# Token rows loaded last, the first x tile scaled in three pieces, a smaller warm-up tile and drawn offsets in the order of a hybrid attention block

## The chip, the cores and the metric

One core of one Trainium2 chip. The metric is the device time of one execution in microseconds; the kernel before has a median of 430.17 us in 3 runs (429.69 to 430.26). Engines are named as in the profile: PE (TensorE's matmuls), PEld (its weight loads), DVE (VectorE), ACT (ScalarE), POOL (GpSimd) and SP (SyncE, which issues most DMAs).

## The reference

The kernel computes one pre-norm residual layer for 512 tokens of width 1024 in float32. With h = rmsnorm(x) * g, one combined projection h @ w_in gives latents, gates and indexer inputs:

```python
h = rmsnorm(x, norm_g[l])
(q_lat, c_kv, k_rope, z_a, q_b, k_b, v_b, z_b,
 q_idx, k_idx, w_idx, gate_a, gate_b) = jnp.split(h @ w_in[l], cuts, axis=-1)
...
merged = (jax.nn.sigmoid(gate_a) * (y_a @ w_o_a[l])
          + jax.nn.sigmoid(gate_b) * (y_b @ w_o_b[l]))
x = x + merged @ w_out[l]
```

Branch a is latent attention: eight heads, queries from a normalised latent of 384 (q_lat), keys and values from one of 256 (c_kv), a shared rotary key, a mask by chunks of 64 tokens. Branch b is attention over selected keys: an indexer of eight small heads scores all keys, each query keeps its 128 best, and a relative position bias is added. Each branch is gated with SiLU, and the sum passes an output projection, the residual and a final rmsnorm.

## The kernel before, in words

**How the order is made.** The work is written as some sixty Python generators ("threads"), each of which yields steps: an engine (or a choice of engines) with an estimated duration, the tiles it writes and those it reads. `Flow.run` (L180) is a list scheduler that runs when the program is built: it keeps a modelled time for each engine, asks for each thread's next step when it could start (`Flow.start`, L163), and emits the step with the smallest key, `s + BIAS * t.prio` with BIAS = 0.01 (L201), ties settled by the thread's priority. What it emits is the fixed order of each engine's queue. On the chip every engine then runs its own queue strictly in that order and waits on semaphores for its inputs. Steps with a choice (DVE or POOL, DVE or ACT) go to the engine that finishes first by the model.

**Precision.** Each product is done as three matmuls of operands split in a high and a low part (`mm3`, L395): high part by a cast (`act`, L305: ACT's CAST at L292, or ACTIVATE at L301 when it scales), low part by a subtraction on DVE or POOL (`lo_part`, L371, at L318 or L320; `split_scaled`, L375, at L329). All matmuls of this kind stand at L390, transposes at L407.

**The start** is where most of the change lies. `setup` (L472) issues the first load of the indexer weight (w_qi, 256 columns) from ACT's queue, writes two constants on DVE (neghalf, and junk with 512 columns) and loads the exponential table. `warm_up` (L481) multiplies junk, read as bfloat16, with itself: seven matmuls of 512 columns. `loads` (L516) issues on SP the eight tiles of x transposed (xT, 128 channels by 512 tokens each, k = 0 to 7), and with them the weights w_qi (256 columns for each k) and w_kvl (328 columns for each k: the kv latent, the indexer key, the rotary key and the indexer's head weights); then the four tiles of w_ql (the q latent). After pair kp = XAT = 1 of xT, that is between k = 3 and k = 4, it stands still for `x_squares` (L552): eight loads of x by token rows (128 tokens by 512 channels), whose squares are summed on ACT (L560, into junk), added in pairs on DVE, and raised to -1/2 on POOL (L368) to give rstd, one number a token. Four transposes on PE (L568) lay rstd along the free dimension, and ACT copies it to rbc (L570).

`early_x` (L595) scales each xT tile by the norm's gain into a high and low part; `early_w` (L603) splits w_qi and w_kvl for each k, then w_ql. `early_mm` (L616) runs on PE for each k six matmuls of 384 columns (the indexer queries, two banks, tokens 128 to 511) and twelve of 328 columns (the kv latents, one bank for each token tile); then the q latents, 96 matmuls of 384 columns. None of these needs rstd, which is applied to the results afterwards: `take_qi` (L716), `latent` (L681). The normalised tiles h (`normed`, L657), on which all other projections run, need rbc, and so do the rope tables' loads on POOL (L496 to L498), which wait for it.

**The rest.** Projections, attention heads, top-k selection (48 pairs of MAX8 and MATCH_REPLACE8 on DVE) and the output products follow, interleaved by the scheduler: a `fetcher` loads weight tiles ahead into four raw buffers, a `splitter` splits them, a `multiplier` fills PE with projections while heads wait for DVE and ACT. Seven strips of products end the kernel (`output`, L1751), followed by the final rmsnorm and eight stores.

Of the kernel before, what the change touches and what calls it, by code (L numbers as in the profile page):

```python
# [2 lines left out]

# [9 lines left out]
BF16 = mybir.dt.bfloat16  # L13
AF = mybir.ActivationFunctionType
# [111 lines left out]


class Thread:
    def __init__(self, gen, prio):
        self.gen, self.prio, self.req, self.alive = gen, prio, None, True  # L130


class Flow:
# [9 lines left out]
    def __init__(self):  # L143
# [3 lines left out]
        self.port = 0.0  # L147
        self.threads = []

    def spawn(self, gen, prio):  # L150
        t = Thread(gen, prio)
        self.threads.append(t)
        self.advance(t, None)
        return t
# [25 lines left out]
    def run(self, stop=None):  # L180
        while self.threads:
            if stop and stop():
                return
            moved = False
            for t in sorted(self.threads, key=lambda t: t.prio):
                if isinstance(t.req, Get):
                    b = t.req.pool.give(t.req)
                    if b is not None:
                        self.advance(t, b)
                        moved = True  # L190
                elif isinstance(t.req, Until) and t.req.cond():
                    self.advance(t, None)
                    moved = True
            if moved:
                continue
            best = None
            for t in self.threads:
                if isinstance(t.req, Step):
                    for i, (eng, dur, emit) in enumerate(t.req.options):
                        s = self.start(t.req, eng)  # L200
                        key = (s + BIAS * t.prio, t.prio)  # L201
                        if len(t.req.options) > 1:
                            fin = s + dur + {"POOL": self.pbias if t.req.pbias is None else t.req.pbias, "ACT": t.req.abias}.get(eng, 0.0)
# [12 lines left out]
            if eng == "SP":  # L216

                self.free["SP"] = s + 0.05
                self.hw = max(self.hw, s) + (0.65 if step.ins and step.outs else 0.475)
                self.dma = max(self.dma, self.hw + 0.65) + dur  # L220
                end = self.dma + (2.2 if step.ins and step.outs else 1.0) + step.late
            else:
                self.free[eng] = end = s + dur
                if self.shares(step, eng):
                    self.port = end
                if step.moves:
                    self.dma = max(self.dma, end + (1.0 if eng == "POOL" else 0.8)) + step.moves
                    end = self.dma + 1.0
            for b in step.ins:
                b.r = b.reads[eng] = max(b.r, end)  # L230
            for b in step.outs:
                b.w = max(b.w, end)
                b.written, b.by = True, eng
            self.advance(t, None)


RAW_LAG = {"DVE": 0.125, "POOL": 0.1, "ACT": 0.1}
BIAS = 0.01
TC_ARGS = {}


@with_exitstack
def tile_block(ctx: ExitStack, tc: tile.TileContext, a: dict, out: bass.AP, bias_dram: bass.AP):
# [211 lines left out]
    kpe = [fixed(f"kpe{c}", [68, S], F32R) for c in "hl"]  # L455
    mask = [fixed(f"mask{i}", [P, P * (i + 1)]) for i in range(NT)]
    junk = fixed("junk", [P, S])
    warm = fixed("warm", [P, 8])
    ss8 = [fixed(f"ss{t}", [P, 2]) for t in range(NT)]
    rstd = fixed("rstd", [P, NT])  # L460
    rb = fixed("rb", [64, NH])
    rbs = fixed("rbs", [64, NH], F32R)
    TOK = [slice(t * P, (t + 1) * P) for t in range(NT)]
    LO, HI = slice(0, 256), slice(256, 512)
    SCORED = slice(P, S)
    SWAP = [(k + 16) % 32 for k in range(32)]
    done = set()

# [3 lines left out]
    def setup():  # L472

        rq = yield slot("er")
        yield act_dma(rq.all.f[:, :256], a["w_qi"][0][:, :256])
        eraw["q", 0] = rq.all.f[:, :256], True
        yield memset("DVE", neghalf.all, -0.5)
        yield memset("DVE", junk.all, 0.0)
        yield act(warm.all, neghalf.all, AF.Exp)

    def warm_up():  # L481

        ps = yield bank("pv")
        z = junk.tile.bitcast(BF16)
        for _ in range(NWARM):
            yield pe(0.43, [ps.all], [junk.all], lambda: nc.tensor.matmul(
                ps.tile, z[:, :P], z[:, :S], start=True, stop=True))
        put(ps)

    def setup_pool():  # L490
# [25 lines left out]
    def loads():  # L516
# [32 lines left out]
                eraw["ql", 2 * kp + c] = r[:, QR * c : QR * c + QR], c == 1  # L549
        done.add("loads")  # L550

    def x_squares():  # L552
        tiles = []

        def squares():
            for t in range(NT):
                for half in range(2):
                    yield Until(lambda: len(tiles) > 2 * t + half)
                    xn = tiles[2 * t + half]
                    yield act(junk.all, xn.all.f, AF.Square, accum=ss8[t][:, half : half + 1])  # L560
                    put(xn)
            ss = yield Get(SMALL)
            for t in range(NT):
                yield tt(ss[:, t : t + 1], ss8[t][:, 0:1], ss8[t][:, 1:2], ALU.add)
# [19 lines left out]
    def split_w(raw, w, dst, key, cls="w", cap=None, release=False, early=False):  # L584
# [7 lines left out]
            put(raw.buf)  # L592
        dst[key] = (hi, lo)

    def early_x():  # L595
        for k in range(NK):
            yield Until(lambda: k in xt)
            hi = yield slot("xg")
            lo = yield slot("xg")
            yield from split_scaled(hi.all, lo.all, xt[k].all.f, normg[:, k : k + 1])  # L600
            xg[k] = (hi, lo)

    def early_w():  # L603
# [12 lines left out]
    def early_mm():  # L616
# [2 lines left out]
            qi_ps.append((yield bank("e")))  # L619
        for _ in range(NT):  # L620
            kv_ps.append((yield bank("e")))
        for k in range(NK):
            yield Until(lambda: k in xg and k in ewq)

# [1 line left out]
            w = [cut(ewq[k], slice(m * P, m * P + P)) for m in range(2)]  # L626
            if k == 0:

                for cw, cx in ((0, 0), (1, 0), (0, 1)):
                    for m in range(2):  # L630
                        yield mm(qi_ps[m][:, SCORED], [(w[m][cw], xk[cx])], not (cw or cx), False)
# [1259 lines left out]
NORM = ('DVE', 'POOL')  # L1891
NORM_B = ('DVE', 'ACT')
NORM_BIAS = -0.5
NWARM = 7
XAT = 1
QPOOL = 1
PHCAP = 8
WCAP = 8
# [95 lines left out]
```

## Time and profile before

| | |
|---|---|
| median of 3 runs | 430.17 us (429.69 to 430.26) |
| the profiled execution's own time | 429.84 us |
| its span, first to last instruction | 428.1 us |
| mean granted TensorE clock | 0.994 |
| busy: PE, DVE, ACT, POOL | 415.9, 379.3, 264.6, 118.7 us |
| DMA | 65.89 MB, mean 154 GB/s |

A row of the timeline gives start, duration, engine, line, operation, tiles written and read, and behind a bracket the idle time of the engine just before and what ended it. In a list of waits the three numbers are the total, the count and the longest. In a table of stages each engine has its busy time and, after an x, its instructions, in the order PE, PEld, DVE, ACT, POOL. A group of instructions has its busy time, then the mean duration of one in ns. Because matmuls overlap, the start-to-start distance of rows says more of PE than a row's length.

### The profile page before, as it was taken

Reading aid. Unit: us, or ns where it says so; the run is one execution under the profiler, and the core shown is the slowest. Engines: PE = TensorE matmul, PEld = TensorE weight load, DVE = VectorE, ACT = ScalarE, POOL = GpSimd, SP = SyncE. Lnnn points to the kernel's source line nnn. Section 1 sums busy time; section 2 is a strip of 40 time slices with the busy share of each in tenths; the row PEclk is TensorE's granted clock in tenths of the full one; section 3 lists DMA queues with packets and bytes.
Section 4 is the critical chain, followed back from the end, with each engine's and each line's share of the span. In section 5 each row is a group of like instructions: output and inputs, shape, how many; then the busy total and the mean of one; then the engine's idle time right before and its main releaser. Section 6 shows DMA issues by size and latency. Waiting matters only on the chain.

```text
span 428.1 us, 7167 instructions
## 1 busy us (share of the span) xinstructions
PE 415.9 (97%) x2303; PEld 363.9 (85%) x2303; DVE 379.3 (89%) x840; ACT 264.6 (62%) x595; POOL 118.7 (28%) x144
## 2 busy tenths in 40 slices
PE   8899999999999999999999999999999999999993
PEld 6899978888888888888799988998998888888882
DVE  4599599999999999999879898988789767999995
ACT  5985876656472676448564678494598534336624
POOL 1247857544545648510000001000010002001112
PEclk9999999999999999999999999999999999999997
DMA  8964334736318630472354435615522887448205
GB/s 261 394 221 155 107 99 128 196 107 171 96 53 229 172 116 3 132 200 99 100 141 144 152 95 136 165 52 177 150 85 80 293 334 253 160 132 278 94 2 196
DMA packets 30277, 65.89 MB, mean 154 GB/s; under 512 B 4648, under 2 KB 5688, under 8 KB 30240
## 3 DMA queue, kind: packets, MB, share of 16 engines
q1 hardware_dynamic: 29264, 64.08, 48.5%
q0 software_dynamic: 832, 1.22, 1.0%
q8 instruction: 18, 0.29, 0.3%
q14 instruction: 19, 0.16, 0.1%
q10 hardware_dynamic: 144, 0.13, 0.1%
HBM read 50.49 MB, written 4.21 MB: 128 GB/s over the span
## 4 chain that ended last, share of the span: by engine, by line
PE 55%; DVE 22%; DMA 8%; ACT 6%; issue 5%; SPq 1%; POOL 1%; POOLq 0%; DVEq 0%; ACTq 0%
PE ps L390 49%; PE ps L407 4%; DMA raw<-w_out 3%; DVE mask L791 3%; DVE sm L790 3%; ACT s_p L301 2%; DVE s_mg L318 2%; DVE s_wsum L318 1%; DMA s_sig<-bias_scratch 1%; DVE sm L1412 1%; DMA raw<-w_kvl 1%; DMA s_op<-kpel 1%; DVE s_wo L318 1%; SPq L417 1%; DVE s_w L318 1%
## 5 line engine op out<-in xcount | busy, mean ns | idle before, releaser
L390 PE MATMUL ps<-s_h,s_w 128*128 128x512 f32 (+1 forms) x732 | 169.9, 379 | 0.0
L390 PEld LDWEIGHTS ps<-s_h,s_w 128*128 128x128 f32 x732 | 127.9, 189 | 22.1 <-DVE s_w L318 0.2
L292 ACT CAST s_w<-raw 128x512 fp32r<-128x512 f32 (+3 forms) x124 | 71.1, 591 | 21.3 <-DVE raw L318 12.5
L320 POOL TENSOR_TENSOR s_w<-raw,s_w 128x512 fp32r<-128x512 f32 (+2 forms) x40 | 50.1, 1263 | 121.5 <-ACT s_w L292 75.9
L318 DVE TENSOR_TENSOR s_w<-raw,s_w 128x512 fp32r<-128x512 f32 (+2 forms) x84 | 54.9, 667 | 8.5 <-ACT s_w L292 8.0
L390 PE MATMUL ps<-s_ys,s_w 128*128 128x512 f32 x192 | 43.7, 389 | 0.0
L390 PEld LDWEIGHTS ps<-s_ys,s_w 128*128 128x128 f32 x192 | 36.0, 188 | 7.5
L390 PE MATMUL ps<-s_w,s_xg 128*128 128x328 f32 (+1 forms) x192 | 32.5, 323 | 0.5 <-DVE s_w L318 0.5
L390 PE MATMUL ps<-s_wo,s_mg 128*128 128x512 f32 (+1 forms) x156 | 33.0, 373 | 0.0
L390 PEld LDWEIGHTS ps<-s_w,s_xg 128*128 128x128 f32 x192 | 31.5, 188 | 0.8 <-DVE s_w L318 0.8
L390 PEld LDWEIGHTS ps<-s_wo,s_mg 128*128 128x128 f32 x156 | 27.6, 188 | 5.2
L301 ACT ACTIVATE s_p<-s_p,sm 128x128 f32<-128x128 f32 (+3 forms) x56 | 29.2, 551 | 3.9 <-DVE sm L1509 3.8
L318 DVE TENSOR_TENSOR s_ph<-ps,s_ph 128x384 fp32r<-128x384 f32 (+1 forms) x48 | 27.0, 592 | 0.6
L301 ACT ACTIVATE s_p<-ps,sm 128x128 f32<-128x128 f32 (+3 forms) x32 | 16.8, 527 | 17.1 <-DVE sm L1412 16.5
L791 DVE MATCH_REPLACE8 mask<-sm,mask 128x256 f32<-128x256 f32 (+2 forms) x48 | 25.8, 540 | 0.0
L790 DVE MAX8 sm<-mask 128x8 f32<-128x256 f32 (+2 forms) x48 | 25.2, 546 | 0.1
L292 ACT CAST s_ph<-ps 128x384 fp32r<-128x384 f32 (+1 forms) x48 | 23.0, 516 | 1.9 <-PE ps L407 1.5
L407 PE MATMUL ps<-ident,s_p 128*128 128x128 f32 x160 | 23.3, 274 | 0.3 <-ACT s_p L301 0.3
L390 PE MATMUL ps<-s_ph,vv 128*128 128x512 f32 (+3 forms) x128 | 23.3, 318 | 0.2 <-DVE s_ph L318 0.2
L390 PEld LDWEIGHTS ps<-s_ph,vv 128*128 128x128 f32 x128 | 20.8, 188 | 2.5 <-DVE s_ph L318 0.4
L351 POOL TENSOR_SCALAR s_p<-s_p,sm 128x128 f32<-128x128 f32 (+3 forms) x32 | 17.3, 544 | 15.6 <-DVE sm L1389 15.4
L407 PEld LDWEIGHTS ps<-ident,s_p 128*128 128x128 f32 x160 | 18.7, 140 | 3.3 <-ACT s_p L301 0.5
(191 smaller groups left out, 750.5 us busy)
## 6 DMA issues: line engine op xcount, KB each, us to landing
raw<-w_out SPq DMA_DIRECT2D x18, 512.0 KB, 4.0
s_op<-s_op SPq DMA_DIRECT2D x36, 128.0 KB, 2.4
raw<-w_ga SPq DMA_DIRECT2D x8, 512.0 KB, 4.5
raw<-w_gb SPq DMA_DIRECT2D x8, 512.0 KB, 4.0
raw<-w_o SPq DMA_DIRECT2D x16, 256.0 KB, 3.7
s_x<-xT SPq DMA_DIRECT2D x8, 256.0 KB, 5.6
s_xn<-x SPq DMA_DIRECT2D x8, 256.0 KB, 5.5
raw<-w_za SPq DMA_DIRECT2D x4, 512.0 KB, 5.0
```

The costliest lines, as they stand in the source:

```text
L292: nc.scalar.copy(dst.ap, src.ap)
L301: nc.scalar.activation(dst.ap, src.ap, func, **kw)
L318: opts.append(("DVE", 0.07 + 0.00104 * x.n, lambda: nc.vector.tensor_tensor(dst.ap, x.ap, y.ap, op=op)))
L320: opts.append(("POOL", 0.15 + 0.0021 * x.n, lambda: nc.gpsimd.tensor_tensor(dst.ap, x.ap, y.ap, op=op)))
L351: lambda: nc.gpsimd.tensor_scalar(dst.ap, x.ap, s.ap, 1.0, ALU.mult, ALU.mult)))
L390: nc.tensor.matmul(ps.ap, l.ap, r.ap, start=start and i == 0, stop=stop and i == len(pairs) - 1, skip_group_check=more)
L407: nc.tensor.transpose(d.ap, s.ap, ident.tile)
L417: return Step([("SP", n / 360000.0, lambda: nc.sync.dma_start(d, s))], bufs(dst), bufs(src))
L790: yield Step([("DVE", t, lambda: nc.vector.max(m8.tile, work.tile))], [m8], [work])
L791: yield Step([("DVE", t, lambda: nc.vector.match_replace(work.tile, m8.tile, work.tile, MARK))], [work], [m8])
L1412: yield Step([("DVE", 0.07 + 0.00104 * n, lambda: nc.vector.tensor_reduce(mx.tile[:, 1:2], ps.tile[:, :n], op=ALU.max, axis=AX.X, negate=T ...
```

## The change

1. `XAT` goes from 1 to 3: the eight token-row loads and what hangs on them stand behind all eight xT tiles with their w_qi and w_kvl loads, and ahead of w_ql.
2. The squares of the token rows may run on ACT or DVE (`square_sum`), each into its own accumulator, over the tile itself in place of junk. In the order that results six run on ACT and two on DVE.
3. The first xT tile is scaled in three pieces (tokens 256 to 511, 128 to 255, 0 to 127) in place of one; the first indexer matmuls (high times high) run by pieces of 256 and 128 columns.
4. The warm-up reads a new tile, zeros, of 128 float32 columns (256 in bfloat16): 15 matmuls of 256 columns in place of 7 of 512; junk is no longer cleared.
5. Each thread gets an offset drawn between 0 and 0.01 (`NUDGE`, seed `DRAW` = 0), added to its key. It changes the order of all queues, and with it which engine some steps with a choice get: over the whole program DVE has 11 instructions more, ACT 4 and POOL 3 fewer. The matmuls are the same but for the warm-up and the split of the first ones.

```diff
-    def __init__(self, gen, prio):
-        self.gen, self.prio, self.req, self.alive = gen, prio, None, True
+    def __init__(self, gen, prio, nudge):
+        self.gen, self.prio, self.nudge, self.req, self.alive = gen, prio, nudge, None, True
...
-        t = Thread(gen, prio)
+        t = Thread(gen, prio, self.draw.random() * NUDGE)
...
-                        key = (s + BIAS * t.prio, t.prio)
+                        key = (s + BIAS * t.prio + t.nudge, t.prio)
...
+    PIECES = (slice(256, S), slice(P, 256), slice(0, P))
...
+        yield memset("DVE", zeros.all, 0.0)
         yield memset("DVE", neghalf.all, -0.5)
-        yield memset("DVE", junk.all, 0.0)
         yield act(warm.all, neghalf.all, AF.Exp)
...
-        z = junk.tile.bitcast(BF16)
+        z = zeros.tile.bitcast(BF16)
         for _ in range(NWARM):
-            yield pe(0.43, [ps.all], [junk.all], lambda: nc.tensor.matmul(
-                ps.tile, z[:, :P], z[:, :S], start=True, stop=True))
+            yield pe(WARM, [ps.all], [zeros.all], lambda: nc.tensor.matmul(
+                ps.tile[:, :256], z[:, :P], z, start=True, stop=True))
...
+    def square_sum(xn, dst):
+
+        x = xn.all.f
+        step = act(x, x, AF.Square, accum=dst.all)
+        step.options.append(("DVE", 0.19 + 0.00104 * x.n, lambda: nc.vector.tensor_tensor_reduce(
+            x.ap, x.ap, x.ap, op0=ALU.mult, op1=ALU.add, scale=1.0, scalar=0.0, accum_out=dst.tile)))
+        step.pair = True
+        return step
...
-                    yield act(junk.all, xn.all.f, AF.Square, accum=ss8[t][:, half : half + 1])
+                    yield square_sum(xn, ss8[t, half])
...
+            if k == 0:
+
+                for piece in PIECES:
+                    yield act(hi[:, piece], xt[k].all.f[:, piece], AF.Copy, scale=normg[:, k : k + 1])
+                    first_x[piece.start] = hi
+                yield stt(lo.all, xt[k].all.f, normg[:, k : k + 1], hi.all.f, ALU.mult, ALU.subtract)
+            else:
+                yield from split_scaled(hi.all, lo.all, xt[k].all.f, normg[:, k : k + 1])
...
+        yield Until(lambda: 0 in ewq)
+        for i, piece in enumerate(PIECES[:2]):
+            yield Until(lambda: piece.start in first_x)
+            for m in range(2):
+                yield mm(qi_ps[m][:, piece], [(ewq[0][0][:, m * P : m * P + P], first_x[piece.start][:, piece])], not i, False)
...
-                for cw, cx in ((0, 0), (1, 0), (0, 1)):
+                for cw, cx in ((1, 0), (0, 1)):
...
-NWARM = 7
-XAT = 1
+NWARM = 15
+WARM = 0.22
+XAT = 3
```

More of the change, by code (lines that the diff above doesn't have):

```diff
@@ L1 @@
 import math
+import random
 from contextlib import ExitStack
@@ L148, in __init__ @@
         self.threads = []
+        self.draw = random.Random(DRAW)
     def spawn(self, gen, prio):
-        t = Thread(gen, prio)
+        t = Thread(gen, prio, self.draw.random() * NUDGE)
         self.threads.append(t)
@@ L238 @@
 BIAS = 0.01
+NUDGE = 0.01
+DRAW = 0
 TC_ARGS = {}
@@ L457, in tile_block @@
     junk = fixed("junk", [P, S])
+    zeros = fixed("zeros", [P, P])
     warm = fixed("warm", [P, 8])
-    ss8 = [fixed(f"ss{t}", [P, 2]) for t in range(NT)]
+    ss8 = {(t, h): fixed(f"ss{t}{h}", [P, 1]) for t in range(NT) for h in range(2)}
     rstd = fixed("rstd", [P, NT])
@@ L563, in squares @@
             for t in range(NT):
-                yield tt(ss[:, t : t + 1], ss8[t][:, 0:1], ss8[t][:, 1:2], ALU.add)
+                yield tt(ss[:, t : t + 1], ss8[t, 0].all, ss8[t, 1].all, ALU.add)
             yield from small_pow(rstd.all, ss[:, :NT], 1.0 / D)
@@ L593, in split_w @@
         dst[key] = (hi, lo)
+    first_x = {}
     def early_x():
@@ L599, in early_x @@
             lo = yield slot("xg")
-            yield from split_scaled(hi.all, lo.all, xt[k].all.f, normg[:, k : k + 1])
+            if k == 0:
[5 more added lines that the diff above has]
+                yield from split_scaled(hi.all, lo.all, xt[k].all.f, normg[:, k : k + 1])
             xg[k] = (hi, lo)
@@ L627, in early_mm @@
             if k == 0:
-                for cw, cx in ((0, 0), (1, 0), (0, 1)):
+                for cw, cx in ((1, 0), (0, 1)):
                     for m in range(2):
-                        yield mm(qi_ps[m][:, SCORED], [(w[m][cw], xk[cx])], not (cw or cx), False)
+                        yield mm(qi_ps[m][:, SCORED], [(w[m][cw], xk[cx])], False, False)
             else:
```

## The prediction

> **What bounds the kernel now.** I read the page first, then who waited for whom on PE, then the timeline of the start, then stages.
>
> ```profile
> span 428.1 us, 7167 instructions
> PE 415.9 (97%) x2303; PEld 363.9 (85%) x2303; DVE 379.3 (89%) x840; ACT 264.6 (62%) x595; POOL 118.7 (28%) x144
> ```
>
> PE is idle for 428.1 - 415.9 = 12.2 us of the span. The waits of PE say where idle time can be won:
>
> ```profile
> PE ps L407 <- POOL rstd L368: 1.8, 1, 1.8
> PE ps L486 <- DVE junk L444: 1.5, 1, 1.5
> PE ps L390 <- DVE s_w L318: 0.5, 1, 0.5
> PE ps L390 <- ACT s_xg L301: 0.3, 1, 0.3
> PE ps L407 <- ACT s_p L301: 0.3, 1, 0.3
> PE ps L1430 <- DMA s_op<-kpel: 0.2, 1, 0.2
> PE ps L390 <- DVE s_ph L318: 0.2, 1, 0.2
> ```
>
> The first four, 4.1 us, lie before 25 us; the last three, 0.7 us, are all that the remaining 400 us hold. The matmuls are the same in both kernels but for the warm-up and two more in the first step, so the time is set by when PE gets going, by how rarely it stops in the first 30 us, and by whether the new order keeps the rest as full. The start:
>
> ```profile
> 0.94 0.48 DVE L444 MEMSET junk<- 128x512 f32 x1
> 1.48 3.17 PE L486 MATMUL ps<-junk 128*128 128x512 bf16 x7 [1.48 <-DVE junk L444]
> 3.90 0.41 ACT L292 CAST s_w<-s_er 128x256 fp32r<-128x256 f32 x1 [1.24 <-DMA s_er<-w_qi]
> 4.22 0.72 ACT L301 ACTIVATE s_xg<-s_x,normg 128x512 fp32r<-128x512 f32 x1
> 4.99 2.15 PE L390 MATMUL ps<-s_xg,s_w 128*128 128x384 f32 x6 [0.34 <-ACT s_xg L301]
> 5.15 0.47 ACT L292 CAST s_w<-s_er 128x328 fp32r<-128x328 f32 x1 [0.22 <-DMA s_er<-w_kvl]
> 5.65 0.50 DVE L318 TENSOR_TENSOR s_w<-s_er,s_w 128x328 fp32r<-128x328 f32 x1
> 6.42 0.72 ACT L301 ACTIVATE s_xg<-s_x,normg 128x512 fp32r<-128x512 f32 x1 [0.80 <-DMA s_x<-xT]
> 6.97 1.96 PE L390 MATMUL ps<-s_w,s_xg 128*128 128x328 f32 x12
> 7.04 0.76 ACT L292 CAST s_w<-s_er 128x256 fp32r<-128x256 f32 x2
> 7.17 0.75 DVE L329 SCALAR_TENSOR_TENSOR s_xg<-s_x,normg,s_xg 128x512 fp32r<-128x512 f32 x1 [1.02 <-ACT s_xg L301]
> 7.84 0.83 DVE L318 TENSOR_TENSOR s_w<-s_er,s_w 128x256 fp32r<-128x256 f32 x2
> 8.77 1.23 PE L390 MATMUL ps<-s_xg,s_w 128*128 128x384 f32 x6
> 9.84 1.95 PE L390 MATMUL ps<-s_w,s_xg 128*128 128x328 f32 x12
> 11.62 1.20 PE L390 MATMUL ps<-s_xg,s_w 128*128 128x384 f32 x6
> ```
>
> A step of the contraction (k) is six matmuls for the indexer and twelve for the kv latents. Undisturbed it takes 11.62 - 8.77 = 2.85 us: 1.07 for the six, 1.78 for the twelve (0.149 each). Step 0 runs its six at 0.33 each, so PE was still at half speed there.
>
> ```profile
> 17.42 0.19 ACT L301 ACTIVATION_READ_ACCUMULATOR junk<-s_xn 128x1 f32 x1
> 17.51 0.71 ACT L301 ACTIVATE s_xg<-s_x,normg 128x512 fp32r<-128x512 f32 x1
> 18.16 1.04 POOL L368 TENSOR_TENSOR rstd<-rstd,neghalf 128x4 f32<-128x4 f32 x1
> 19.17 0.63 POOL L421 DMA_DIRECT2D ropec<-ropec  x1
> 19.26 0.65 PE L407 MATMUL ps<-ident,rstd 128*128 128x128 f32 x4 [1.83 <-POOL rstd L368]
> 19.67 1.31 PE L390 MATMUL ps<-s_xg,s_w 128*128 128x384 f32 x6
> 22.25 0.72 ACT L301 ACTIVATE s_xg<-s_x,normg 128x512 fp32r<-128x512 f32 x1
> 24.49 1.93 PE L390 MATMUL ps<-s_w,s_xg 128*128 128x328 f32 x11 [0.52 <-DVE s_w L318]
> 30.13 12.17 PE L390 MATMUL ps<-s_w,s_xg 128*128 128x328 f32 x71
> ```
>
> Here the eight loads of x's token rows and their eight squares stand between steps 3 and 4: ACT reaches the fifth x tile only at 17.51, PE waits 1.83 us and later 0.52. The last row starts with the twelve matmuls of step 7, at 30.13.
>
> **The change part by part.** *Token rows behind the other loads (XAT 3).* Steps 1 to 6 and the first six matmuls of step 7 take 6 x 2.85 + 1.07 = 18.17 us of PE. In the trace they take 30.13 - 8.77 = 21.36. Of the 3.19 us between, the four transposes of rstd stay (19.67 - 19.26 = 0.41 of PE); **2.78 us of stalls go**, if the loads of steps 4 to 7 keep ahead of PE, and they do: with eight loads and eight squares less in front of them each comes earlier than before.
>
> What is late next is rstd itself. In the new order its transposes stand in PE's queue after the six matmuls of step 6. The same bytes lie ahead of the last token tile as lay ahead of the last x tile, which had landed at 22.25 at the latest. A square (0.54 to its accumulator read) and the tail from that read to PE (19.26 - 17.42 = 1.84) give rstd at 22.25 + 0.54 + 1.84 = 24.6. PE comes there at about 25.3 (below). So the wait is hidden with 0.7 us to spare, and each 0.1 us beyond that would be paid in full. The loads of w_ql stay behind the token tiles; on POOL the two rope loads and the mask rows wait for rstd and move from 19.17 to about 26 us, still long ahead of the rope at 53.84 (its row stands below). Two of the eight squares go to DVE.
>
> ```profile
> L1509 DVE CUSTOM_DVE_ANT_0 s_p<-ps,s_p 128x512 f32<-128x512 f32 x8 | 5.4, 674 | 0.0
> 24.00:50.00 26.00, 25.51 (x154) 25.38 (x155) 21.74 (x38) 19.05 (x47) 16.65 (x21) 1.00 0.44 133
> 70.00:200.00 130.00, 129.60 (x683) 110.93 (x682) 128.96 (x331) 77.34 (x186) 67.10 (x78) 1.00 0.48 133
> 48.56 1.03 PE L407 MATMUL ps<-ident,s_latraw 128*128 128x128 f32 x8
> 53.84 0.68 DVE L318 TENSOR_TENSOR s_tmp<-ps,ropec 32x512 f32<-32x512 f32 x1
> ```
>
> By the first row two such reductions cost DVE 1.4 us, before 23 us, where it has holes. Then everything that needs rstd or its broadcast starts some 6 us later (transposes at 25.4 instead of 19.26): the eight normalised tiles, the kv latents. Their first user on PE comes after the w_ql matmuls, at 48.56 before and about 47 now. DVE has 26 - 21.74 = 4.3 us free between 24 and 50; the splits of steps 4 to 7 leave that stretch (about 3.3 us) and about as much enters (two more low parts of h, one of th, scalings moved over from POOL). I take 0 for this, with 2 us to spare, and keep 0 to +2.
>
> *First x in pieces.* This one loses. ACT's order is now, from the program:
>
> ```
> Activation warm, Activation s_xg 128x256, Activation s_xg 128x128 x2, TensorCopy s_w<-s_er(w_qi) 128x256,
> Activation s_xg<-s_x(second x tile) 128x512, TensorCopy s_w<-s_er(w_kvl) 128x328
> DVE: low part of x 0, of w_qi 0, of x 1, of w_kvl 0
> ```
>
> Both pieces of the first matmuls need the weight, and its cast now stands behind all three pieces. From the rows a column costs (0.47 - 0.41) / 72 = 0.0008 us, so three pieces in place of one add two fixed parts, some 0.4 us, and the weight that was cast from 3.90 is cast from about 5.1: PE's first real matmul starts near 5.6 instead of 4.99. That is not yet the price. The kv weight's cast now stands behind the second x tile, which starts at 6.42 because it lands only then. So the cast runs from 7.04 to 7.5 instead of from 5.15, and on DVE its low part stands behind the low part of x 1: it can start at 7.84, where the next row starts now, and takes 0.50. The second of the twelve matmuls needs it: 8.34 + 0.06 = 8.4, where now it starts at 6.97 + 0.15 = 7.12. Step 1 then starts at 8.4 + 11 x 0.149 = 10.04 instead of 8.77: **1.27 us lost**. PE reaches the rstd transposes at 10.04 + 5 x 2.85 + 1.07 = 25.36.
>
> *Warm-up from a smaller tile.* Seven matmuls of 512 columns at 0.427 become 15 of 256 at about 0.214: 3.2 us instead of 3.0, starting some 0.35 us earlier, since a memset of 128 columns replaces the one of 512 that takes 0.48. All of it lies before the first real matmul; taken as 0. The row behind it: PE needed from 1.48 to about 6.9 us of matmuls, with one hole of 0.34, until its full speed came (0.33 us a matmul of 384 columns at 4.99, 0.149 for 328 at 6.97). Now holes of about 1.2 us (4.4 to 5.6) and 0.8 us (7.6 to 8.4) lie in that stretch. The Trainium skill, "TensorE: Matmul & The Clock Gate", Part 1, says that the clock stays at half until a free-running window of some 3.4 us has been busy; by that rule the holes can fail a window, which one with the trace's single hole did not; the trace agrees that half speed comes first and lasts some microseconds (1.48 to 6.9). By the trace alone the sum has 0 here; by the rule it has between 0 and 1.7 us (an estimate: half speed for one window more).
>
> *Drawn offsets.* Each thread's key gets up to 0.01 us, which reorders all five queues after the start. DVE gets 11 more instructions, ACT and POOL 4 and 3 fewer; the last 36 matmuls and the stores keep their order. One w_out load moves behind the final x and gain tiles:
>
> ```profile
> 388.71 2.02 SPq L417 DMA_DIRECT2D s_fg<-final_g  x2
> 414.92 5.83 PE L390 MATMUL ps<-s_wo,qhi 128*128 128x512 f32 x36
> ```
>
> It is issued near 391, and the product that it feeds ends only at 414.92, over 20 us later: hidden. What it can win is the 0.7 us of late waits; what it can lose is bounded by DVE, full from 70 to 200 us (128.96 of 130): about 2 us of work more there would be 2 us of PE. I take 0 as nearest the rows, since PE has hardly a wait in either stretch, and keep -0.7 to +2.
>
> **Sum:** -2.78 + 1.27 = -1.51 us against the profiled execution's 429.84 us (span 428.1 and 1.7 around it): 428.3 us. The profiled execution lies 0.33 under the median of the runs, 430.17, so 428.3 to 428.7; I say 428.4.
>
> **The rivals.** (a) *The clock.* If the holes make PE's count start over at 8.4, full speed comes as long after that as it came after the first warm-up (1.48 to 6.9, 5.4 us), and half of those 5.4 us is lost: -1.5 + 2.7 = +1.2, 431.0 us, slower. It decides if the two holes weigh more than the 0.34 us that was tolerated; against it, 1.2 + 0.8 us in 7 is still little. By the page's window the price is smaller: one window more, +1.7 by its figure, would give about 430.0. Chance 0.15. (b) *The cover is gone:* the work behind rstd, 6 us later, makes PE wait at 47 to 50 us, or rstd itself comes after 25.4; price 1 to 2 us, net about 0, 429.8. For it: DVE is busy for 21.74 of 26 us there. Against: the 4.3 us left. Chance 0.2. (c) *More is won:* the late waits go, and the second x tile lands earlier than 6.42 so that the start loses nothing: -2.8, 427.0. Against: its place in SP's queue is the same. Chance 0.15.
>
> **How the numbers follow.** Forecast 0.5. About 0.2% (0.86 us) is what a measurement here can tell from no change. Faster holds 0.9 of the forecast and (c): 0.45 + 0.15 = 0.60; same the rest of the forecast, most of (b) and a little of (a): 0.23; slower what is left of (a) and (b): 0.17. The range reaches from (c) with a little more to (a): 426.5 to 431.0.
>
> **What would show it.** Right: PE's first real matmul near 5.6 and a hole in PE before 8.4 released by the DVE split of w_kvl; no wait over 0.3 us at steps 4 to 7; the transposes of rstd near 25.4 with no wait; the twelve matmuls of step 7 at about 28.6. Wrong: a start of step 1 away from 10.0; a wait of PE on POOL rstd; matmuls of 328 columns at 0.27 us after 8.4 (a); waits of PE on s_h or s_latraw at 47 to 50 us (b); new waits of PE of over 1 us after 50.

## The result and the profile after

The changed kernel takes **428.08 us** (median of 20 runs, 427.14 to 430.56) against 430.0 us for the kernel before on the same chip (20 runs, 429.5 to 430.98): ratio 0.996, 95% interval 0.995 to 0.997. It is faster by 1.9 us; 428.4 was forecast.

The profiled execution is the slowest of those 20: 430.56 us, span 428.8, mean granted clock 0.991. It is read for where PE waits, not for its length. First the page, then the waits of PE (total, count, longest):

```profile
span 428.8 us, 7187 instructions
PE 416.8 (97%) x2313; PEld 365.4 (85%) x2313; DVE 379.1 (88%) x851; ACT 261.1 (61%) x589; POOL 120.2 (28%) x141
```

```profile
PE ps L395 <- ACT s_w L297: 1.5, 2, 1.3
PE ps L493 <- DVE neghalf L449: 1.1, 1, 1.1
PE ps L395 <- DMA qhi<-s_op: 0.7, 1, 0.7
PE ps L395 <- ACT s_pair L297: 0.7, 1, 0.7
PE ps L412 <- DVE s_p L353: 0.7, 1, 0.7
PE ps L395 <- DVE s_w L323: 0.5, 2, 0.3
PE ps L395 <- DVE s_pair L323: 0.5, 1, 0.5
```

The wait for rstd (1.8 us before) is gone. What is new at the start is the wait for the cast of the first weight; what is new later are four waits of 0.5 to 0.7 us behind 190 us, 2.6 us where the kernel before had 0.7 (whether they belong to the order or to this execution is seen below, with 24 warm-ups). The timeline of PE at the start, and the stretch around rstd:

```profile
1.05 3.38 PE L493 MATMUL ps<-zeros 128*128 128x256 bf16 x15 [1.05 <-DVE neghalf L449]
5.72 0.68 PE L395 MATMUL ps<-s_xg,s_w 128*128 128x256 f32 x4 [1.28 <-ACT s_w L297]
...
7.77 0.52 PE L395 MATMUL ps<-s_w,s_xg 128*128 128x328 f32 x1 [0.25 <-ACT s_w L297]
8.61 3.14 PE L395 MATMUL ps<-s_w,s_xg 128*128 128x328 f32 x11 [0.32 <-DVE s_w L323]
11.59 1.21 PE L395 MATMUL ps<-s_xg,s_w 128*128 128x384 f32 x6
...
25.73 1.21 PE L395 MATMUL ps<-s_xg,s_w 128*128 128x384 f32 x6
26.77 0.60 PE L412 MATMUL ps<-ident,rstd 128*128 128x128 f32 x4
27.13 2.05 PE L395 MATMUL ps<-s_w,s_xg 128*128 128x328 f32 x12
29.01 1.21 PE L395 MATMUL ps<-s_xg,s_w 128*128 128x384 f32 x6
30.06 1.20 PE L395 MATMUL ps<-s_w,s_xg 128*128 128x328 f32 x7
```

The steps now follow each other without a hole: step 1 at 11.59, step 6 at 25.73, step 7's twelve at 30.06. That is 18.47 us for what took 21.36 before. But step 1 starts 2.8 us later than before (8.77), and of the eleven matmuls at 8.61 each took (11.59 - 8.61) / 11 = 0.271 us instead of 0.149. The stretch in the table of stages, whose last three numbers are the granted clock, the DMA share and GB/s:

```profile
7.90:11.30 3.40, 3.08 (x11) 2.74 (x12) 2.99 (x7) 2.59 (x6) 0.00 (x0) 0.50 1.02 388
```

The clock was at half here. This is the forecast's rival (a), in this execution at least.

### The profile page after: what moved, and what is told of

Same layout as the page of the kernel before. It is cut to its first block, busy times and chain, and to the rows that moved or that the text cites. A ratio compares the mean times of both kernels' runs of the same rounds, so it can differ in the third digit from the quotient of the medians.

```text
span 428.8 us, 7187 instructions
## 1 busy us (share of the span) xinstructions
PE 416.8 (97%) x2313; PEld 365.4 (85%) x2313; DVE 379.1 (88%) x851; ACT 261.1 (61%) x589; POOL 120.2 (28%) x141
## 4 chain that ended last, share of the span: by engine, by line
PE 74%; DVE 13%; DMA 4%; ACT 4%; issue 2%; POOL 0%; SPq 0%; POOLq 0%; ACTq 0%; DVEq 0%
PE ps L395 66%; PE ps L412 4%; DVE s_w L323 2%; ACT s_p L306 2%; DMA raw<-w_gb 2%; DVE s_ph L323 1%; ACT s_w L297 1%; DMA qhi<-qhi 1%; DMA s_x<-xT 1%; DVE raw L323 1%; PE ps L798 1%; DVE s_tmp L323 1%; PE ps L1461 1%; PE ps L1460 1%; DVE s_y L323 1%
## 5 line engine op out<-in xcount | busy, mean ns | idle before, releaser
L395 PE MATMUL ps<-s_h,s_w 128*128 128x512 f32 (+1 forms) x732 | 169.7, 378 | 0.7 <-ACT s_pair L297 0.7
L395 PEld LDWEIGHTS ps<-s_h,s_w 128*128 128x128 f32 x732 | 127.9, 189 | 22.8 <-ACT s_pair L297 0.9
L297 ACT CAST s_w<-raw 128x512 fp32r<-128x512 f32 (+3 forms) x124 | 71.7, 593 | 24.6 <-DVE raw L323 15.9
L325 POOL TENSOR_TENSOR s_w<-raw,s_w 128x512 fp32r<-128x512 f32 (+2 forms) x38 | 46.0, 1214 | 106.8 <-ACT s_w L297 105.3
L323 DVE TENSOR_TENSOR s_w<-raw,s_w 128x512 fp32r<-128x512 f32 (+2 forms) x86 | 58.2, 689 | 5.7 <-ACT s_w L297 4.9
L395 PE MATMUL ps<-s_ys,s_w 128*128 128x512 f32 x192 | 43.7, 389 | 0.0
L395 PEld LDWEIGHTS ps<-s_ys,s_w 128*128 128x128 f32 x192 | 36.0, 188 | 7.5
L395 PE MATMUL ps<-s_w,s_xg 128*128 128x328 f32 (+1 forms) x192 | 34.0, 333 | 0.6 <-DVE s_w L323 0.3
L395 PEld LDWEIGHTS ps<-s_w,s_xg 128*128 128x128 f32 x192 | 32.5, 195 | 1.2 <-DVE s_w L323 0.7
L395 PE MATMUL ps<-s_wo,s_mg 128*128 128x512 f32 (+1 forms) x156 | 33.0, 373 | 0.0
L395 PEld LDWEIGHTS ps<-s_wo,s_mg 128*128 128x128 f32 x156 | 27.6, 188 | 5.2
L306 ACT ACTIVATE s_p<-s_p,sm 128x128 f32<-128x128 f32 (+3 forms) x53 | 27.5, 541 | 7.2 <-DVE sm L1539 6.1
L325 POOL TENSOR_TENSOR s_p<-s_bias,mask 128x384 f32<-128x384 f32 (+1 forms) x5 | 4.3, 886 | 78.1 <-DVE s_w L323 71.8
L297 ACT CAST s_ph<-ps 128x384 fp32r<-128x384 f32 (+1 forms) x48 | 23.8, 521 | 4.0 <-PE ps L412 3.8
L821 DVE MATCH_REPLACE8 mask<-sm,mask 128x384 f32<-128x384 f32 (+2 forms) x48 | 25.8, 542 | 0.0
L820 DVE MAX8 sm<-mask 128x8 f32<-128x384 f32 (+2 forms) x48 | 25.5, 548 | 0.1
L395 PE MATMUL ps<-s_ph,vv 128*128 128x512 f32 (+3 forms) x128 | 25.4, 324 | 0.0
L412 PE MATMUL ps<-ident,s_p 128*128 128x128 f32 x160 | 23.8, 273 | 0.7 <-DVE s_p L353 0.7
L395 PEld LDWEIGHTS ps<-s_ph,vv 128*128 128x128 f32 x128 | 20.4, 189 | 1.8
```

The costliest lines, as they stand in the source:

```text
L297: nc.scalar.copy(dst.ap, src.ap)
L306: nc.scalar.activation(dst.ap, src.ap, func, **kw)
L323: opts.append(("DVE", 0.07 + 0.00104 * x.n, lambda: nc.vector.tensor_tensor(dst.ap, x.ap, y.ap, op=op)))
L325: opts.append(("POOL", 0.15 + 0.0021 * x.n, lambda: nc.gpsimd.tensor_tensor(dst.ap, x.ap, y.ap, op=op)))
L395: nc.tensor.matmul(ps.ap, l.ap, r.ap, start=start and i == 0, stop=stop and i == len(pairs) - 1, skip_group_check=more)
L412: nc.tensor.transpose(d.ap, s.ap, ident.tile)
```

## The experiments

**Theory A** (of the prediction): the stalls that go at steps 3 and 4 are worth 2.8 us, the start's new order costs 1.3, the rest is as full as it was, the draw is worth nothing. **Theory B**: the order of the work behind rstd decides; it was planned for an early rstd, and the draw happens to give one that bears a late one. **Theory C**: the clock's fall at the start hides part of the gain. (In some expectations below, R says that the late rows pay in any order that is held fixed, M that a late rstd makes waits of its own in an order made for an early one.)

### One part at a time

The kernel before with late token rows alone:

```diff
-XAT = 1
+XAT = 3
```

> The kernel before with XAT = 3 alone: no pieces, old warm-up, no drawn offsets; the start's order on ACT is that of before (w_qi, x 0, w_kvl, x 1). My theory (the gain is the stalls between steps 3 and 4 that go, 2.8 us; the start's new order costs 1.3 of it): about 2.5 to 2.8 us under before, 427.2 to 427.5 us, step 7's kv matmuls near 27.4 us, lower than the changed kernel itself by 0.5 to 1. Rival (the drawn order gives the gain, not the loads): within 0.9 us of before.

Measured: 432.43 us (7 runs) against 430.39, ratio 1.0053 (1.0034 to 1.0073): slower by 2, which neither side had expected. The stalls at steps 3 and 4 are gone in its trace too, step 7's twelve start at 28.39 (30.13 before). The gain is given back later, most of it in waits of PE that the kernel before doesn't have, two from 71.9 and 77.5 us on VectorE, two from 211.6 and 217.1 us on ScalarE:

```profile
PE ps L768 <- DVE mask L329: 1.4, 1, 1.4
PE ps L407 <- ACT s_p L301: 1.2, 2, 0.9
...
PE ps L768 <- DVE s_op L329: 0.5, 1, 0.5
```

The changed kernel without the draw:

```diff
-NUDGE = 0.01
+NUDGE = 0.0
```

> The changed kernel with NUDGE = 0. Its order starts with w_qi ahead of the x pieces and w_kvl ahead of x 1, so it also lacks the start's loss. My theory (draw worth about 0, start's order worth 1.3): 426.8 to 427.8 us, at or below the changed kernel. Rival (the drawn order is what gained): above the changed kernel's 428.1, 429 or more.

Measured: 436.26 us (4 runs), ratio 1.0133 (1.0117 to 1.0149). So the edit that I had taken at nothing is worth some 8 us beside the others (5.9 over its kernel before here, 1.9 under it with the draw). Its start is the better one (step 7's twelve at 28.57); its waits of PE come later, some ten of 0.2 us and more, among them:

```profile
PE ps L412 <- ACT s_p L306: 2.0, 4, 0.8
PE ps L412 <- DVE mask L342: 1.4, 1, 1.4
PE ps L395 <- POOL s_w L325: 1.2, 1, 1.2
```

The changed kernel with a warm-up that lasts until the weight is cast (the planned durations are scaled, so that every other instruction keeps its place):

```diff
-NWARM = 15
-WARM = 0.22
+NWARM = 24
+WARM = 0.22 * 15 / 24
```

> The changed kernel with 24 warm-up matmuls in place of 15, planned with the same total time, so that every queue keeps its order: the hole of 1.3 us on PE ahead of the first real matmul is filled. Clock theory (the holes at the start make the clock fall back in some executions, which spreads the times from 427.1 to 430.6): median 0.4 to 0.8 lower, 427.3 to 427.7, few or no times over 429, no fall of the clock in the profile. Rival (the spread has nothing to do with the start): same median and spread; if the first matmul, now near 6.2 instead of 5.7, counts in full: 0.5 higher.

Measured: 428.2 us (12 runs, 427.26 to 430.74), ratio 0.9951 (0.9936 to 0.9966). In its trace the clock doesn't fall, step 1 starts at 10.37, 1.2 us earlier than in the changed kernel's trace, and still median and spread are nearly the same. The median is 2.2 us under the kernel before on its chip, that of the changed kernel 1.9, and the intervals overlap. Theory C is not borne out; a price of a few tenths of a us is not excluded. VectorE, ScalarE and GpSimd run the same order here as in the changed kernel, and PE but for the nine more warm-up matmuls. Of the four late waits only the one for s_p is left (0.7), and by the starts of the same matmuls PE is 0.8 us ahead of the changed kernel's trace at 180 us and 3.1 ahead at 240. So the other three don't come with the order; they belong to that execution, the slowest of its 20.

Pieces and warm-up, without the moved rows and without the draw:

```diff
-NUDGE = 0.01
+NUDGE = 0.0
...
-XAT = 3
+XAT = 1
```

> The kernel before with the pieces, the new warm-up and the squares' choice, but XAT = 1 and no drawn offsets; nearly all of the order of before stays, and w_qi is cast ahead of the x pieces. My theory (pieces and warm-up are worth nearly nothing when the order of the start is good): 429.6 to 430.2 us, within 0.4 of before. Rival (an earlier warm-up brings full speed earlier, or the pieces start PE earlier): 0.5 to 1 lower.

Measured: 430.37 us (12 runs), ratio 1.0001 (0.9986 to 1.0016). These parts do nothing that can be measured.

No part alone is faster: late rows cost 2, pieces and warm-up give 0, and together without the draw they cost 6. Only with the draw is there a gain.

### Orders kept fixed

With any edit the planner makes a new order for the whole program, so late rows had been compared in other orders than before. For the next kernels its choices are read from a list: which thread's step comes next, on which engine. The list of one kernel can be followed from any place on with the start of another, and then only what the edit moves changes its place. The list takes 87 lines, so that L390 of the kernel before is L477 there, and L395 of the changed kernel L482:

```diff
-            best = None
-            for t in self.threads:
...
+            t, s, eng, dur, emit = self.listed()
             emit()
```

Late rows in the order of the kernel before (on PE only the four transposes of rstd move):

> The kernel before, with the token rows loaded behind the last x and w loads and their squares behind step 7's casts (XAT = 3), but every later instruction in the order that the kernel before has (the planner's choices are read from a list; on PE only the transposes of rstd change their place). In the run with XAT = 3 alone, whose later order the planner made anew, PE was 1.7 us ahead of the kernel before at 30 us (by the work it had done) and 2.5 us behind it at the end. Theory R (the move is worth 1.7 us, and what was lost later was lost by the new order): 428.3 to 428.9 us against 430.2 to 430.4 for the kernel before, with no wait of PE over 1 us between 50 and 400 us. Rival M (the move itself, by work behind rstd that comes 6 us later, makes the later waits): 430 to 433, with waits of PE at 50 to 90 us again.

Measured: **435.47 us** (4 runs), ratio 1.0129 (1.0114 to 1.0144). My theory R in that expectation, that the move pays in the old order, is refuted by 7 us; rival M is what happens, at more than the 430 to 433 that I gave it. PE in its trace, and VectorE behind it:

```profile
50.99 1.64 PE L477 MATMUL ps<-s_h,s_w 128*128 128x512 f32 x6
55.80 0.90 PE L855 MATMUL ps<-s_qs,s_qs 96*128 96x256 f32 x2 [3.18 <-DVE s_qs L405]
56.50 2.76 PE L477 MATMUL ps<-s_h,s_w 128*128 128x512 f32 x6
```

```profile
52.41 1.32 DVE L435 TENSOR_SCALAR s_latraw<-ps,rstd 128x384 f32<-128x384 f32 x2 [2.31 <-ACT junk L388]
...
55.07 0.68 DVE L405 TENSOR_TENSOR s_qs<-ps,s_qs 32x512 fp32r<-32x512 f32 x1
```

PE waits 3.18 us for the index queries, s_qs, which VectorE finishes at 55.7; and then six matmuls of 512 columns take 2.76 us instead of 1.64, for the clock has fallen:

```profile
56.00:60.00 4.00, 4.00 (x13) 3.31 (x14) 3.43 (x6) 1.31 (x3) 3.62 (x5) 0.50 0.30 92
```

The same place in the kernel before:

```profile
49.00 1.32 DVE L348 TENSOR_SCALAR s_latraw<-ps,rstd 128x384 f32<-128x384 f32 x2 [2.72 <-ACT junk L301]
...
51.57 0.68 DVE L318 TENSOR_TENSOR s_qs<-ps,s_qs 32x512 fp32r<-32x512 f32 x1
```

```profile
52.66 0.46 PE L768 MATMUL ps<-s_qs,s_qs 96*128 96x256 f32 x2
```

There s_qs was ready at 52.25 and PE came at 52.66: 0.4 us of cover. VectorE was already waiting 2.7 us, for ScalarE's squares of the latents, which stand on ScalarE behind the casts of h, which need rstd. Neither engine's list shows this as a wait of PE; one sees it only by comparing when an operand is ready with when PE takes it. With rstd's broadcast 6.2 us later (26.15 instead of 19.95) s_qs comes 3.5 us later, and PE at 52.62, as before.

Because PE has the same order in both, the price can be followed from matmul to matmul. With late rows PE is 2.67 us ahead at step 7 (27.46 instead of 30.13) and level at 52.6; it starts the first product of s_qs 3.14 us behind (55.80 instead of 52.66), is 6.0 behind when the clock is back (61.9 us), and 5.7 at the last matmul. So the wait makes one half of the price and the slow clock the other, and PE loses nothing more after that.

Half the move, same order:

```diff
-XAT = 1
+XAT = 2
```

> The kernel before with the token rows loaded after the loads of step 5 (XAT = 2, halfway between before and the change), every later instruction in the order of the kernel before. With the rows after step 7's loads (XAT = 3) in that same order, PE waited 3.2 us at 52 us for VectorE's q parts, which stand there behind work that needs rstd, and its clock fell for a while after it: 435.5 us. Theory M (an order made for an early rstd pays for each us that rstd comes later, beyond the slack it has): rstd some 3 us earlier than with XAT = 3, so a wait at 52 us of under 1 us, no fall of the clock, and 429 to 431 us. Rival: what costs is that the rows move at all (their squares among step 6's and 7's casts), then 433 or more here too.

Measured: 432.92 us (6 runs), ratio 1.0071 (1.0055 to 1.0087). The broadcast of rstd comes at 23.43, and:

```profile
53.61 0.56 PE L855 MATMUL ps<-s_qs,s_qs 96*128 96x256 f32 x2 [2.69 <-DVE s_qs L405]
```

I had expected a wait under 1 us and no fall of the clock, since I counted only how much later VectorE is (1.3 us) and not that PE, freed of the start's stalls, gets there 1.7 us earlier (53.61 - 2.69 = 50.92). The clock fell too, for one stretch from 54.76 to 58.17 us. By the number alone the rival (433 or more) was nearer. What speaks for theory M is the trace, with the same wait at the same place, and that the cost goes with the move: 0, +2.8, +5.6 us for rows after step 3, step 5, step 7. My number was wrong.

All of the change but the draw, in the order of the kernel before behind rstd:

> All of the change but the draw (token rows late, x in pieces, 15 small warm-up matmuls), with every instruction behind rstd in the order that the kernel before has. Theory R: as the kernel before's order with the move alone, 428.2 to 428.9, some 8 us under the same change with an order made without a draw (436.3), and 0.5 to 1 over the drawn order, whose end is 1 us shorter. Rival M: 430 or more.

Measured: 433.83 us (6 runs), ratio 1.0098 (1.0071 to 1.0125). It waits 3.2 us at the same place. And the other way round, the drawn order with the rows early (the start as with pieces and warm-up alone):

> The fourth cell of the square of two orders by two places of the token rows: the pieces, the small warm-up and the drawn order behind rstd, but the token rows loaded after step 3's loads as in the kernel before (XAT = 1). The start then has the stalls of the kernel before (PE 1.5 us later at 30 us than with the rows late and the weights first). Theory: the drawn order is better by itself and doesn't need the late rows: 428.5 to 429.5, between before (430) and e7_weights_first (428.1). Rival: the drawn order fits the late rows alone and has waits of its own with rows early: 430.5 or more.

Measured: 430.26 us (11 runs), ratio 0.9998 (0.9986 to 1.001), outside both ranges and nearer to the rival's. In its trace the execution ends 8.1 us behind the last matmul (9.4 with pieces and warm-up alone), but the last matmul itself ends 2.05 us later (422.15 against 420.10); 1.2 of these are there at step 7 (31.24 against 30.02), where x tiles landed later (the third is scaled from 8.82 us on instead of 7.84). That completes a square (ratio to the kernel before; all four have the pieces and the small warm-up):

| | rows after step 3 | rows after step 7 |
|---|---|---|
| order made without a draw, or that of before | 1.0001 | 1.0098 (before's order), 1.0133 (made anew) |
| drawn order | 0.9998 | 0.996 |

The draw alone gives nothing, the late rows without the draw cost 4 to 6 us (2 and 5.6 without the pieces and the warm-up, in an order made anew and in before's), both together gain 1.9. Neither has a price of its own. How the drawn order bears it is seen on ScalarE and VectorE: although the broadcast of rstd comes at 27.41 in the changed kernel's trace, ScalarE's squares of the q latents start at 45.65 (45.30 before, 49.14 with late rows in before's order). The same eight casts of h stand ahead of them, but between the broadcast and the squares ScalarE is idle for 3.5 us instead of 8.6 with late rows in before's order, where it waits 4.3 us in front of two s_oh for a tile that GpSimd loads and the rest mostly for VectorE. And s_qs is there when PE comes:

```profile
47.79 2.46 DVE L353 TENSOR_SCALAR s_latraw<-ps,rstd 128x384 f32<-128x384 f32 x4
...
51.25 0.68 DVE L323 TENSOR_TENSOR s_qs<-ps,s_qs 32x512 fp32r<-32x512 f32 x1 [0.28 <-ACT s_qs L297]
```

VectorE no longer waits in front of the latents. What it has done by 80 us differs with the orders (stretch, busy time and instructions of VectorE, clock, DMA). Kernel before; late rows in its order; changed kernel:

```profile
0.00:80.00 80.00, 62.05 (x109) 1.00 0.61 193
```

```profile
0.00:80.00 80.00, 56.28 (x101) 0.96 0.55 181
```

```profile
0.00:80.00 80.00, 65.47 (x124) 0.98 0.61 198
80.00:150.00 70.00, 69.84 (x208) 1.00 0.49 129
```

In before's order, 5.8 us of VectorE's work fewer by 80 us go with 6.0 us more at the end (435.82 against 429.84 us in the profiled executions). The changed kernel is ahead of before by 3.4 us, 1.4 of them for two squares that ScalarE did before. From 80 to 150 us VectorE is full in all three (69.65, 69.72 and 69.84 of 70), so what it lacks at 80 isn't made up there. This goes for a delay inside one order; it doesn't rank the orders. Made anew without a draw, VectorE has done 63.37 us by 80 us, and with the second seed below 65.08, both more than the kernel before, and these kernels take 6 and 7 us longer.

Another seed:

```diff
-DRAW = 0
+DRAW = 1
```

> The changed kernel with another seed for the offsets (DRAW = 1 instead of 0), nothing else. If the draw of the changed kernel was a lucky one among orders that the planner holds for equal, this one lies between it and the order without a draw: 430 to 436. If offsets as such help, whatever they are: 427.5 to 428.7.

Measured: 437.01 us (5 runs), ratio 1.0155 (1.0135 to 1.0175). This order also changes what is computed (which operand is at fault wasn't traced; the instructions are the same in kind and nearly in number, so only its time is read, with that reserve). It lies above the 430 to 436 of the lucky draw, and far above the other range. By this run another draw is 9 us off the first: offsets as such do not help; this set of them does.

### Can the start's gain be had as well?

The changed kernel's order, but the weights ahead: on ScalarE and VectorE the cast of w_qi 0 before x 0, and that of w_kvl 0 before x 1.

> The changed kernel with its own order in all but the start: ACT casts w_qi 0 ahead of the three pieces of x 0, and w_kvl 0 ahead of x 1 (VectorE likewise); all else stands where it stood. If the start's order costs what its trace shows (first real matmul at 5.7 instead of 4.7 us, the first step's second group at 8.6 instead of 7.4), PE is some 1 us ahead after step 0 and the holes that set the clock back are gone: 426.6 to 427.4 us against 428.0 for the changed kernel, with fewer of its executions above 428. Rival: the time is set by later waits whatever the start does, 427.8 to 428.3.

Measured: 428.09 us (12 runs, 426.27 to 429.97), ratio 0.9955 (0.994 to 0.9969). The time is the rival's, though the start is as wanted: no fall of the clock, PE reaches the transposes at 23.8 instead of 26.77. There it now waits, since rstd can't be earlier:

```profile
25.20 0.65 PE L499 MATMUL ps<-ident,rstd 128*128 128x128 f32 x4 [1.39 <-POOL rstd L460]
```

So these transposes were put nine matmuls later:

> The kernel with the weights cast first at the start and the drawn order behind it (e7_weights_first), with the four transposes of rstd placed three kv groups (nine matmuls of 328 columns, some 1.4 us) later on PE, and the copy of their result behind them. There PE waited 1.4 us for rstd at 23.8 us. If that wait took the start's gain: no wait there, PE 1.2 to 1.4 us further on from 30 us to the end, 426.6 to 427.2 us. Rival (VectorE and ScalarE behind rstd decide, PE would only wait later): 427.7 to 428.3, with a new wait of PE behind 40 us.

Measured: 428.22 us (6 runs), ratio 0.995 (0.9937 to 0.9962). That wait is gone; the one for s_p at 278 us stays, and new ones stand at 51 and 272 us, as the rival had it:

```profile
PE ps L499 <- DVE s_p L440: 1.0, 1, 1.0
PE ps L482 <- ACT s_pair L384: 0.6, 1, 0.6
...
PE ps L885 <- DVE s_qs L410: 0.5, 1, 0.5
```

And then the transposes of s_p at 278 us, nine matmuls later too:

> As e11_turn_later, and in the same way the transposes of s_p at 277 us, where PE waited 1.0 us for VectorE's scaling, behind three gate groups (nine matmuls of 256 columns, 1.1 us) that followed them. If no wait is waiting behind it, 1.0 us less than e11_turn_later: 425.6 to 426.3. Rival: VectorE's end of the work is set elsewhere, no difference to e11_turn_later.

Measured: 428.1 us (6 runs), ratio 0.9949 (0.9936 to 0.9963): no difference, the rival again. The wait at 278 us is gone, and two matmuls that read s_ph at 281 and 282 us come 0.4 and 0.5 us later than their pace. Four ways of giving PE a lead, one result (the first score product is the first matmul that reads s_qs):

| profiled execution | PE at the first score product | end of the last matmul | own time | median |
|---|---|---|---|---|
| before | 52.66 | 420.75 | 429.84 | 430.0 |
| changed | 52.57 | 422.45 | 430.56 | 428.08 |
| 24 warm-ups | 51.76 | 419.32 | 427.42 | 428.2 |
| weights first | 51.04 | 419.30 | 427.41 | 428.09 |
| and rstd's transposes later | 51.47 | 420.36 | 428.46 | 428.22 |
| and s_p's transposes later | 50.81 | 420.34 | 428.43 | 428.1 |

In the last four rows PE reaches the score products over a range of 0.95 us, and neither the last matmul nor the median follows it. VectorE's full stretch from 80 to 150 us does not take the lead: against the version with 24 warm-ups, the one with the weights first is 0.7 us ahead on PE and on VectorE alike from 60 to 150 us. At 260 us 0.66 of it are left, at 280 nothing. The stretch between, first with 24 warm-ups, then with the weights first:

```profile
268.33 0.68 DVE L323 TENSOR_TENSOR s_w<-raw,s_w 128x512 fp32r<-128x512 f32 x1
268.93 0.69 DVE L323 TENSOR_TENSOR raw<-raw 128x512 f32<-128x512 f32 x1
269.17 1.73 POOL L325 TENSOR_TENSOR s_p<-s_bias,mask 128x128 f32<-128x128 f32 x2 [6.34 <-DMA s_bias<-bias_scratch]
```

```profile
267.58 1.88 POOL L412 TENSOR_TENSOR s_p<-s_bias,mask 128x128 f32<-128x128 f32 x2 [5.72 <-DMA s_bias<-bias_scratch]
267.65 0.95 DVE L410 TENSOR_TENSOR s_w<-raw,s_w 128x512 fp32r<-128x512 f32 x1
268.52 1.49 DVE L410 TENSOR_TENSOR raw<-raw 128x512 f32<-128x512 f32 x1
```

With the weights first GpSimd's s_p runs beside these two instructions of VectorE, and they take 2.44 us instead of 1.37; a later one takes 0.69 instead of 1.09, so 0.67 is lost on VectorE, as much as the lead. In the last two versions the two take 0.95 and 1.49 us too. That GpSimd is what slows them was not tested by itself. No version tried beats the changed kernel by more than the intervals.

## Why the prediction came out right

The number was right and the sign too, but in part by luck: two steps of its sum were wrong, each by more than the whole gain, and cancelled.

- *Stalls at steps 3 and 4, -2.78.* Right: steps 1 to 6 and the six matmuls behind take 18.47 us, transposes included; 18.17 + 0.41 had been reckoned.
- *rstd ready at 24.6, hidden with 0.7 to spare.* The time was right, and the reserve thin as said. POOL's last step on it in the changed kernel:

```profile
23.72 1.04 POOL L373 TENSOR_TENSOR rstd<-rstd,neghalf 128x4 f32<-128x4 f32 x1
```

  It ends at 24.76. PE came only at 26.77, so nothing was paid; with the weights first PE came at 23.8 and paid 1.39.
- *Start's order, +1.27.* First matmul at 5.72 (5.6 forecast), the second kv matmul at 8.61 (8.4). With 24 warm-ups, where the clock holds, step 1 starts at 10.37 (10.04): the loss is 1.6. The mechanism is as described. That it counts at the end is not: undone, the median stays; in the trace PE loses the lead again between 260 and 280 us.
- *Warm-up, 0, with a rule by which it could be up to 1.7.* In the profiled execution the clock did fall, for one stretch; it cost 11 x (0.271 - 0.149) = 1.3 us, not the 2.7 that rival (a) had by the trace, and within that 1.7. In the median it doesn't show beyond the intervals.
- *Work behind rstd 6 us later, 0 (0 to +2).* **This step failed.** In the old order the late rows cost 5.6 us (4.0 with the rest of the change) in spite of the stalls that they remove, far beyond the range that I kept: 3.2 us of wait at 52 us, and behind it 6.83 us at half clock. I had compared sums (4.3 us free on VectorE from 24 to 50 us) where the order in the queues decides: the chain of h, squares of the latents, s_qs had 0.4 us of cover, and VectorE's free time was a wait inside that chain. Rival (b) named this mechanism and its place, 47 to 50 us, at a price of 1 to 2.
- *Drawn offsets, 0 (-0.7 to +2).* **Failed too**, on the other side: with late rows the draw is worth 5.9 us against the old order and 7.8 against the order made anew without it (each by its distance to the kernel before on its chip); with early rows nothing, to within some 0.5. I priced it by the waits that it could take away from the kernel before, not by those that the rest of the change would have made without it.
- *Not in the sum:* the drawn order ends better. From the last matmul to the end of the execution the drawn orders take 8.1 to 8.3 us, with early or late rows, where orders without a draw take 9.1 to 10.0. In the kernel before VectorE is behind there: its last read of a product starts at 421.97, 1.2 us after the last matmul (420.75); in the changed kernel 0.2 after it (422.45):

```profile
421.97 0.41 DVE L329 SCALAR_TENSOR_TENSOR s_xr<-ps,s_xr 128x256 f32<-128x256 f32 x1
```

```profile
422.67 0.42 DVE L334 SCALAR_TENSOR_TENSOR s_xr<-ps,s_xr 128x256 f32<-128x256 f32 x1
```

So by the trace with 24 warm-ups, the changed order undisturbed, the gain of 2.4 us between these two executions (1.9 to 2.2 between the medians) is made of 0.9 up to the first score product, 0.5 from there to the last matmul and 1.0 behind it, where the prediction had 1.5 at the start and nothing after it.

## What to carry to other kernels

Where every engine runs a queue in a fixed order, delaying a value is priced by following what is queued behind its first user to the next place where the busiest engine needs a result, and by comparing there when it is ready with when it is taken; free time summed over a stage says nothing of it. Two edits to such a program need not add: measure them in the square of with and without, with the rest of the order held fixed, before giving either a price. A scheduler that holds orders for equal (here by 0.01 us) can make ones that lie 8 us apart (436.26 and 428.08), so a part that is tried alone with a newly made order measures mostly the new order.

## What the runs showed of the hardware

PE's clock fell after gaps much shorter than I had thought. The records of the granted clock show that each stretch between two changes is a whole number of 3.413 us (at full speed 47.79 us or 14 of them with late rows in before's order, 51.20 or 15 with all of the change in that order, 416.43 or 122 in the kernel before). A gap of 2.69 us and one of 3.16 each brought one such stretch at half speed, one of 3.18 us two (there the border fell into the gap, at 55.06 us); the start of the changed kernel, with 1.8 us of matmuls in the 3.4 us from 4.5 to 7.9, brought one. In the kernel before the gap of 1.83 us at 17.4 us brought none. The Trainium skill, "TensorE: Matmul & The Clock Gate", Part 1, has the free-running window of 3413 ns, and the records agree: full speed begins between 4.0 and 9.7 us after the first instruction in the 14 traces. The rule of the Trainium skill in the same part (section on HAM oscillation) is that PE be left no gap above about 3.4 us; here gaps of 2.69 us and more were enough, and the measurement decides.

One can lay the borders of these windows through all 14 traces, ends of the kernels included, and add up PE's idle time in each. Every window at full speed in which PE was idle for 1.90 us or more by the profile was followed by half speed (1.90, 2.26, 2.44 and 3.12 us among them), and none with 1.83 or less, but for the changed kernel's start, where 1.6 was enough. The fall comes at the end of such a window. Why the start differs stays open.
